# SyncE's loads in the order of their due times: a planner that lets transfers share one rate, on a four-phase transformer trunk

## The chip, the cores and the metric

The kernel runs on one core of a Trainium2 chip. The metric is the device time of one execution in microseconds (us). Before the change it is 1756.66 us, the median of three runs (1755.53 to 1757.88).

The core has five engines, which run side by side and wait for each other by semaphores: TensorE (PE in the profile; PEld is its loading of weights), VectorE (DVE), ScalarE (ACT), GpSimd (POOL) and SyncE (SP). Here SP computes nothing: it issues the loads of weights, one after the other. When a load has to wait for its buffer, every load behind it on SP waits too.

## The reference

The input x is 512 tokens of 1024 features. Two layers each apply an FFN at half weight, a mixer and another FFN at half weight; the mixer is gated linear attention (GLA) in layer 0 and stick-breaking attention (SB) in layer 1. At the end there is one more RMSNorm.

```python
def swiglu(h, w_gate, w_up, w_down):
    return (jax.nn.silu(h @ w_gate) * (h @ w_up)) @ w_down

for i in range(DEPTH):      # 2
    x = x + 0.5 * swiglu(rmsnorm(x, ffn1_norm[i]), ffn1_w_gate[i], ffn1_w_up[i], ffn1_w_down[i])
    h = rmsnorm(x, mix_norm[i])
    y = gla_mixer(h, ...) if i % 2 == 0 else sb_mixer(h, ...)
    x = x + y
    x = x + 0.5 * swiglu(rmsnorm(x, ffn2_norm[i]), ffn2_w_gate[i], ffn2_w_up[i], ffn2_w_down[i])
return rmsnorm(x, final_norm)
```

w_gate and w_up are 1024x2816, w_down is 2816x1024, all fp32. Four FFNs of 34.6 MB each, the mixers' weights and x make up the 175 MB that the kernel reads.

## The kernel before

**Data.** x stays in SBUF, transposed, as eight tiles x0 to x7 of 128 features x 512 tokens. Weights are loaded in fp32, most in chunks of 1 MB: `raw` (8x256 columns of 128 rows, or 4x512) for gate, up and the mixers, `rawd` (4x256 or 2x512, 512 KB) for the down projections. Each of these two names has two buffers: a load can go out once the tile two before it has been read for the last time.

**Products.** A product in fp32 precision is made of three faster ones. ACT casts a weight to its high part (`wh`, L527), DVE subtracts to get the low part (`wl`, L528), and TensorE adds up wh times the input's high part, wl times the high part and wh times the low part. Inputs are cut the same way (`nh`/`nl`, `hh`/`hl`, `xh`/`xl`, `th`/`tl`). Many products use a scheme of seven instead of eight block products (`seven`, L1069, for gate and up; `seven_down`, L736, for the down projection). It needs sums of weight blocks, made by DVE: `s12` and `s34` (L1079, L1080, L1085, L1086 from raw; L756, L757, L763, L764 from rawd). For the down projection DVE adds what TensorE has accumulated (`ps_w`, `ps_z`, `ps_q`) to x by L778; L727 does so for a plain down projection. TensorE can write on into a bank only after such a read. L950 makes the low part `sl` of the sum of squares of a norm, from which TensorE makes `ps_R` (L469).

**Program order and planned order.** The code emits instructions in an order of its own; a `Feed` walks through the products and calls `Chunk.load` (L486) for chunks ahead, by `nc.sync.dma_start` (L494). At the end a `Planner` (L49) sets a new order of each engine's instructions. `gather` (L81) collects instructions, what each depends on, and buffers; `price` (L171) gives each a duration (`cost`) and the time after which the engine can take the next (`step`). `due` (L271) works backwards from TensorE's instructions to a latest time (`late`) for every other instruction. `run` (L305) then plays the program forward: of all engines it takes the instruction that can start first and puts it at the end of that engine's list. For DVE and ACT the instruction is the one with the least `late` among those that can start by then; TensorE takes its program order, with a little skipping. SP and POOL keep the order of the program: `lists` holds it, and `choose` looks only at its head. `pin` (L55) keeps instructions of one engine in the order in which they are pinned. `begin`, at the start of the program, loads x and the first weights by SP (L2021, L2025, L2030).

The computed times only set orders. On the chip an instruction starts when its engine reaches it and its semaphores allow.

Of the kernel before, what the change touches and what calls it, by code (L numbers as in the profile page):

```python
# [48 lines left out]
class Planner:  # L49
# [5 lines left out]
    def pin(self, ins):  # L55
        e = str(ins.ins.engine)
        if e in self.pinned:
            self.behind_.append((self.pinned[e], ins.ins.name))
        self.pinned[e] = ins.ins.name
        return ins  # L60
# [110 lines left out]
    def price(self, i, kind, e, sizes, psum_in):  # L171
        n = max((s[1] for s in sizes), default=1)
        if e == "PE":
            types = [s[2] for s in sizes]
            if any("bfloat16" in t for t in types):
                return 270.0, max(64.0, 0.43 * n)
            if any("float32r" in t for t in types):
                return 165.0 + 0.42 * n, max(112.0, 0.422 * n)
            moving = sizes[0][1]
            full = sizes[1][1] == P and not kind.endswith("Transpose") and not getattr(i, "is_transpose", False)  # L180
            return 150.0 + 0.9 * n, max(58.0, 0.845 * moving) * (2 if full and moving in (1, P) else 1)
        if "DMA" in kind:
            total = max((s[1] * s[3] for s in sizes), default=1) * 4
            return 2000.0 + total / 400.0, 0.0
        scalars = sum(1 for s in sizes[:-1] if s[1] == 1 and n > 1)
        if e == "DVE":
            reads = [s for s in sizes[:-1] if s[1] > 1]
            if "Scan" in kind:
                n *= 2
            elif len(reads) == 1 and not psum_in and n > 256:  # L190
                n *= 0.5
            return 148.0 + 1.045 * n + 60.0 * scalars, 0.0
        if e == "Activation":
            if "Load" in kind:
                return 1290.0, 0.0
            return 190.0 + 0.835 * n + 95.0 * scalars - 30.0 * psum_in, 0.0
        return 200.0 + n, 0.0
# [107 lines left out]
    def run(self):  # L305
        self.gather()
        late = self.due()
        n = len(self.eng)
        left = [len(self.pred[k]) + self.held[k] for k in range(n)]
        ready, done = [0.0] * n, [None] * n  # L310
# [3 lines left out]
        got = set()  # L314
        clock = dict.fromkeys(ENGINES, 0.0)
        open_ = {e: set() for e in ENGINES}
        lists = {e: [k for k in range(n) if self.eng[k] == e] for e in ("SP", "Pool")}
        out = {e: [] for e in ENGINES}
        for k in range(n):
            if not left[k]:  # L320
                open_[self.eng[k]].add(k)
        shift = 0.0
        back = {"DVE": 80.0, "Activation": 100.0}

        def start(k):
# [13 lines left out]
        def choose(e):  # L339
            now = clock[e]  # L340
            if e in lists:
                if not lists[e] or left[lists[e][0]]:
                    return None
                s = start(lists[e][0])
                return None if s is None else (max(now, s), lists[e][0])
            if e == "PE":
                best = None
                for k in sorted(open_[e])[:60]:
                    s = start(k)
                    if s is not None:  # L350
                        if s <= now + 30.0:
                            return max(now, s), k
                        if best is None or s < best[0]:
                            best = (s, k)
                return best
            able = [(s, k) for k in open_[e] for s in (start(k),) if s is not None]
            if not able:
                return None
            t0 = max(now, min(able)[0])
            s, k = min((x for x in able if x[0] <= t0 + 1.0), key=lambda x: (late[x[1]], x[1]))  # L360
            d = self.cost[k] - back.get(e, 0.0)
            soon = [
                x for x in able
                if t0 + 1.0 < x[0] < t0 + 0.6 * d and late[x[1]] + shift < t0 + d and late[x[1]] < late[k]
            ]
            if soon:
                s, k = min(soon, key=lambda x: (late[x[1]], x[1]))
            return max(now, s), k

        for _ in range(n):  # L370
            best = None
            for e in ENGINES:
                c = choose(e)
                if c is not None and (best is None or c[0] < best[0]):
                    best = (*c, e)
            s, k, e = best
            out[e].append(k)
            open_[e].discard(k)
            if e in lists:
                lists[e].pop(0)  # L380
            end = done[k] = s + self.cost[k]
            if e == "PE":
                clock[e] = s + self.step[k] + (104.0 if s > clock[e] + 20.0 else 0.0)
                shift = s - late[k]
            elif "DMA" in type(self.ins[k]).__name__:
                clock[e] = s + (60.0 if e == "Activation" else 500.0)
            else:
                clock[e] = end - back.get(e, 0.0)
            for t in self.tiles[k]:
                c = self.tag[t]  # L390
                if t not in got:
                    got.add(t)
                    given[c] += 1
                    if used[c] < self.bufs[c]:
                        used[c] += 1
                    else:
                        heapq.heappop(freed[c])
                users[t] -= 1
                ends[t] = max(ends.get(t, 0.0), end)
                if not users[t]:  # L400
                    heapq.heappush(freed[c], ends[t])
            for b in self.succ[k]:
                if not e == self.eng[b] == "PE":
                    ready[b] = max(ready[b], end + self.lag(k, b))
            for b in self.succ[k] + self.after[k]:
                left[b] -= 1
                if not left[b]:
                    open_[self.eng[b]].add(b)
# [27 lines left out]
def decoder(ctx: ExitStack, tc: tile.TileContext, a: dict, out: bass.AP):  # L436
    nc = tc.nc
# [1556 lines left out]
    def begin(ip):  # L1994


        pin = plan.pin
# [14 lines left out]
        x0 = ip.tile([P, 4, NT, 256], F32, name="x0")  # L2012
        entries = {"g": feed.q[0], "u": feed.q[1], "q": feed.q[2]}
        raw = {}
# [3 lines left out]

        def load_x(qr):
            rows = a["x"][0].rearrange("(i p) d -> p i d", p=P)  # L2020
            nc.sync.dma_start(x0[:, qr], rows[:, :, qr * 256 : qr * 256 + 256])  # L2021

        def load_w(nm, hf):
            k = slice(hf * 4, hf * 4 + 4)
            nc.sync.dma_start(raw[nm][:, k], entries[nm].units[0][0].src[:, k])  # L2025

        load_x(0), load_w("g", 0), load_w("u", 0), load_x(1)
        load_x(2), load_w("g", 1), load_x(3), load_w("u", 1)
        for c in phases[0].lead[2:]:
            nc.sync.dma_start(c.t, c.src)  # L2030
        gains(1, ("mix_norm", "ffn2_norm", "gla_o_norm"))


# [141 lines left out]
        done = set()  # L2175
# [61 lines left out]
    with tc.tile_pool(name="ip", bufs=1) as ip:  # L2237
        begin(ip)
# [47 lines left out]
```

## Time and profile before

| | |
|---|---|
| median of three runs | 1756.66 us (1755.53 to 1757.88) |
| profiled execution, its own time | 1758.69 us |
| its span, first to last instruction | 1756.9 us |
| granted TensorE clock | 0.999 |
| PE busy | 1743.7 us, 99% |
| PEld busy | 1635.7 us, 93% |
| DVE busy | 1583.9 us, 90% |
| ACT busy | 1079.4 us, 61% |
| DMA queue of SP (q1) | 175.91 MB, 31.9% of 16 engines' time |

The profile is one execution with every instruction's start and end. A row such as `L528 DVE TENSOR_TENSOR wl<-raw,wh 128x1024 ... x241 | 255.4, 1062 | 50.1` gives line, engine, operation, tiles out and in (without their numbers), shape and count; then busy time in us, mean duration in ns, and the engine's idle time just before. In a timeline, the first two numbers are start and duration in us, and a bracket at the end gives idle time before the instruction and what ended it. A row of waits gives who waited for what: us in total, times, the longest one. For SP the time of an entry is the time of its issue alone, or, for several merged, from the first issue to the last. A row of DMA issues ends with the us from issue to landing. A row of windows gives a stretch, its length, each engine's busy time, the clock, the share of the DMA engines, and GB/s. The four FFNs take about 0 to 310, 520 to 850, 850 to 1170 and 1400 to 1750 us; GLA and SB lie between.

### The profile page before, as it was taken

To read this page: it belongs to the slowest core of one execution; us is meant where nothing else is said; L and a number is where in the kernel's file an instruction comes from. 1 tells how busy PE (TensorE), PEld (TensorE's weight loads), DVE (VectorE), ACT (ScalarE), POOL (GpSimd) and SP (SyncE) were. 2 spreads that over 40 slices of the span, in tenths; PEclk is the share of its full clock that TensorE was granted. 3 is DMA by queue.
4 is the path that set the end of the run, shared out by engine and by line. 5 is a ranking of instruction groups with operands and counts; after the bars stand their busy time and mean duration, and the time that the engine had idled before them with its cause. 6 is when DMAs were issued, how large, how long until landed. Compare 5 with 4: busy or idle time off the path is not lost.

```text
span 1756.9 us, 32000 instructions
## 1 busy us (share of the span) xinstructions
PE 1743.7 (99%) x13002; PEld 1635.7 (93%) x13002; DVE 1583.9 (90%) x2688; ACT 1079.4 (61%) x1906; POOL 9.9 (1%) x24
## 2 busy tenths in 40 slices
PE   9999999999999999999999999999999999999998
PEld 8999999899888899999989999999888888999997
DVE  8999999787888999999899999996898669899996
ACT  7556655545656566565656566566889755555655
POOL 0000000100000000000000000000000000000000
PEclk9999999999999999999999999999999999999999
DMA  6422423421233323333423324242222233233342
GB/s 192 132 85 73 150 85 116 142 73 51 72 96 96 120 71 122 116 101 121 140 75 98 126 92 132 85 132 73 61 73 74 71 96 120 83 111 118 100 132 73
DMA packets 178760, 179.30 MB, mean 102 GB/s; under 512 B 4082, under 2 KB 170276, under 8 KB 178612
## 3 DMA queue, kind: packets, MB, share of 16 engines
q1 hardware_dynamic: 177760, 175.91, 31.9%
q8 instruction: 102, 1.67, 0.4%
q0 software_dynamic: 608, 1.05, 0.3%
q14 instruction: 46, 0.38, 0.1%
q10 hardware_dynamic: 244, 0.29, 0.0%
HBM read 175.17 MB, written 2.10 MB: 101 GB/s over the span
## 4 chain that ended last, share of the span: by engine, by line
PE 78%; DVE 15%; DMA 2%; ACT 2%; issue 2%; DVEq 0%; ACTq 0%; SPq 0%
PE ps_w L1094 17%; PE ps_f L469 14%; PE ps_d L469 9%; PE ps_q L1094 9%; PE ps_w L772 5%; DVE wl L528 5%; PE ps_t L469 5%; PE ps_z L1094 4%; PE ps_b L469 4%; PE ps_q L772 3%; DVE x L778 2%; PE ps_z L1774 1%; PE ps_z L772 1%; DMA rawd<-in_ffn_w_down_dram 1%; PE ps_S L469 1%
## 5 line engine op out<-in xcount | busy, mean ns | idle before, releaser
L528 DVE TENSOR_TENSOR wl<-raw,wh 128x1024 fp32r<-128x1024 f32 x241 | 255.4, 1062 | 50.1 <-ACT wh L527 49.4
L527 ACT CAST wh<-s 128x1024 fp32r<-128x1024 f32 x192 | 201.6, 1051 | 141.2 <-DVE s L1080 38.3
L527 ACT CAST wh<-raw 128x1024 fp32r<-128x1024 f32 x241 | 221.7, 921 | 77.2 <-PE ps_f L469 26.7
L1094 PE MATMUL ps_w<-th,wh 128*128 128x256 f32 x864 | 238.3, 276 | 0.0
L528 DVE TENSOR_TENSOR wl<-s,wh 128x1024 fp32r<-128x1024 f32 x192 | 234.4, 1222 | 3.7 <-ACT wh L527 3.7
L1094 PE MATMUL ps_w<-th,wl 128*128 128x256 f32 x864 | 237.6, 275 | 0.0
L1094 PE MATMUL ps_w<-tl,wh 128*128 128x256 f32 x864 | 237.6, 275 | 0.0
L469 PE MATMUL ps_f<-xh,wh 128*128 128x512 f32 x432 | 166.4, 385 | 0.0
L1094 PEld LDWEIGHTS ps_w<-th,wh 128*128 128x128 f32 x864 | 165.8, 192 | 0.3
L1094 PEld LDWEIGHTS ps_w<-tl,wh 128*128 128x128 f32 x864 | 165.9, 192 | 0.0
L1094 PEld LDWEIGHTS ps_w<-th,wl 128*128 128x128 f32 x864 | 165.9, 192 | 0.0
L469 PE MATMUL ps_f<-xl,wh 128*128 128x512 f32 x432 | 163.7, 379 | 0.0
L469 PE MATMUL ps_f<-xh,wl 128*128 128x512 f32 x432 | 163.7, 379 | 0.0
L469 PE MATMUL ps_d<-hl,wh 128*128 128x512 f32 x288 | 109.4, 380 | 1.4 <-DVE hl L1192 1.4
L469 PE MATMUL ps_d<-hh,wh 128*128 128x512 f32 x288 | 109.8, 381 | 0.4 <-ACT hh L1191 0.2
L469 PE MATMUL ps_d<-hh,wl 128*128 128x512 f32 x288 | 109.2, 379 | 0.0
L527 ACT CAST wh<-rawd 128x512 fp32r<-128x512 f32 (+1 forms) x108 | 80.7, 766 | 20.9 <-PE ps_d L469 12.0
L528 DVE TENSOR_TENSOR wl<-rawd,wh 128x512 fp32r<-128x512 f32 (+1 forms) x108 | 92.9, 866 | 0.3 <-ACT wh L527 0.3
L469 PEld LDWEIGHTS ps_f<-xl,wh 128*128 128x128 f32 x432 | 81.6, 189 | 11.5
L469 PEld LDWEIGHTS ps_f<-xh,wh 128*128 128x128 f32 x432 | 81.7, 189 | 11.0
L469 PEld LDWEIGHTS ps_f<-xh,wl 128*128 128x128 f32 x432 | 81.7, 189 | 10.7
L1094 PE MATMUL ps_q<-th,wh 128*128 128x256 f32 x288 | 79.3, 275 | 0.0
(349 smaller groups left out, 5566.1 us busy)
## 6 DMA issues: line engine op xcount, KB each, us to landing
raw<-in_ffn_w_gate_dram SPq DMA_DIRECT2D x43, 1024.0 KB, 5.4
raw<-in_ffn_w_up_dram SPq DMA_DIRECT2D x43, 1024.0 KB, 5.6
rawd<-in_ffn_w_down_dram SPq DMA_DIRECT2D x84, 512.0 KB, 6.3
raw<-in_gla_w_in_dram SPq DMA_DIRECT2D x12, 1024.0 KB, 5.3
raw<-in_sb_w_in_dram SPq DMA_DIRECT2D x16, 512.0 KB, 3.9
raw<-in_gla_w_out_dram SPq DMA_DIRECT2D x4, 1024.0 KB, 5.1
raw<-in_sb_w_in_dram SPq DMA_DIRECT2D x4, 1024.0 KB, 5.1
raw<-in_sb_w_out_dram SPq DMA_DIRECT2D x4, 1024.0 KB, 5.9
```

The lines of the kernel that those rows point to most:

```text
L469: nc.tensor.matmul(ps, l, r, start=first, stop=last)
L527: nc.scalar.copy(h[:, k], part)
L528: nc.vector.tensor_tensor(out=l[:, k], in0=part, in1=h[:, k].bitcast(F32), op=ALU.subtract)
L772: st["pe"] = nc.tensor.matmul(ps, l_, r_, start=first and c + n == 0, stop=c == 1 and n == 2, skip_group_check=True).ins
L778: nc.vector.scalar_tensor_tensor(out=x, in0=ps, scalar=0.5, in1=x, op0=ALU.mult, op1=ALU.add)
L1094: st["pe"] = nc.tensor.matmul(o, l_, r_, start=first and j + n == 0, stop=j == 3 and n == 2, skip_group_check=True).ins
L1774: nc.tensor.matmul(o_, l_, r_, start=first, stop=last, skip_group_check=True)
```

## The change

Three things change in the planner, and the loads of `begin` are pinned.

- `price` gives a DMA of n bytes 2050 + n/318 ns instead of 2000 + n/400, and a step of n/318 ns instead of none. For 1 MB the cost goes from 4.6 us to 5.3 us.
- `run` lets SP's transfers share one rate: a load is done at the later of its own start plus cost and the end of the load before it plus its step (`bus`).
- `choose` takes for SP, as for DVE and ACT, the load with the least due time among those that can start. SP is no longer in `lists`; POOL is.
- The loads of x and of the first weights are pinned, so that their order stays.

```diff
         if "DMA" in kind:
             total = max((s[1] * s[3] for s in sizes), default=1) * 4
-            return 2000.0 + total / 400.0, 0.0
+            return 2050.0 + total / 318.0, total / 318.0
...
-        lists = {e: [k for k in range(n) if self.eng[k] == e] for e in ("SP", "Pool")}
+        lists = {"Pool": [k for k in range(n) if self.eng[k] == "Pool"]}
...
-        shift = 0.0
+        shift = bus = 0.0
...
             t0 = max(now, min(able)[0])
+            if e == "SP":
+                s, k = min((x for x in able if x[0] <= t0 + 1.0), key=lambda x: (late[x[1]], x[1]))
+                return max(now, s), k
...
             end = done[k] = s + self.cost[k]
+            if e == "SP":
+                end = done[k] = max(end, bus + self.step[k])
+                bus = end
...
-            nc.sync.dma_start(x0[:, qr], rows[:, :, qr * 256 : qr * 256 + 256])
+            pin(nc.sync.dma_start(x0[:, qr], rows[:, :, qr * 256 : qr * 256 + 256]))
...
-            nc.sync.dma_start(raw[nm][:, k], entries[nm].units[0][0].src[:, k])
+            pin(nc.sync.dma_start(raw[nm][:, k], entries[nm].units[0][0].src[:, k]))
...
-            nc.sync.dma_start(c.t, c.src)
+            pin(nc.sync.dma_start(c.t, c.src))
```

The program has the same instructions as before on every engine; their order differs. Of 232 entries on SP, 80 stand where they stood. Of DVE's 2685, 2183 do, of ACT's 1901, 1640, of TensorE's 12637, 12327. The order among the raw loads, and among the rawd loads, is kept; how the two are interleaved is new. In the changed file lines from 391 on stand six further down, so L494 becomes L500 and L778 becomes L784.

On SP in the first FFN, where four rawd loads in a row are followed by the raw loads of the next two chunks (numbers after the names tell tiles apart), before:

```order
L494 DMA raw_1083<-in_ffn1_w_gate_dram 128x8x256
L494 DMA rawd_1167<-in_ffn1_w_down_dram 128x4x256
L494 DMA rawd_1307<-in_ffn1_w_down_dram 128x4x256
L494 DMA rawd_1312<-in_ffn1_w_down_dram 128x4x256
L494 DMA rawd_1420<-in_ffn1_w_down_dram 128x4x256
L494 DMA raw_1425<-in_ffn1_w_up_dram 128x8x256
L494 DMA raw_1555<-in_ffn1_w_gate_dram 128x8x256
L494 DMA raw_1685<-in_ffn1_w_up_dram 128x8x256
```

and on SP at the same place after the change:

```order
L500 DMA raw_1083<-in_ffn1_w_gate_dram 128x8x256
L500 DMA rawd_1167<-in_ffn1_w_down_dram 128x4x256
L500 DMA raw_1425<-in_ffn1_w_up_dram 128x8x256
L500 DMA rawd_1307<-in_ffn1_w_down_dram 128x4x256
L500 DMA raw_1555<-in_ffn1_w_gate_dram 128x8x256
L500 DMA rawd_1312<-in_ffn1_w_down_dram 128x4x256
L500 DMA rawd_1420<-in_ffn1_w_down_dram 128x4x256
L500 DMA rawd_1954<-in_ffn1_w_down_dram 128x4x256
L500 DMA rawd_2075<-in_ffn1_w_down_dram 128x4x256
L500 DMA raw_1685<-in_ffn1_w_up_dram 128x8x256
```

raw_1425 and raw_1555 moved ahead of three and two rawd loads, and the next pair of rawd loads ahead of raw_1685. The other FFN stretches with seven-product down projections look alike.

On DVE in the last FFN, about 1534 to 1542 us of the profile, where the sums of a pair of rawd loads are followed by adds to x, before:

```order
L528 TENSOR_TENSOR wl_18102<-s34_18027,wh_18101 128x1024
L756 TENSOR_TENSOR s12_18107<-rawd_18105 128x512
L763 TENSOR_TENSOR s34_18155<-rawd_17997,rawd_18105 128x512
L757 TENSOR_TENSOR s12_18107<-s12_18107,rawd_17997 128x512
L528 TENSOR_TENSOR wl_18220<-rawd_17997,wh_18219 128x512
L778 SCALAR_TENSOR_TENSOR x4_85<-ps_q_18176,x4_85 128x256
L778 SCALAR_TENSOR_TENSOR x0_81<-ps_w_18158,x0_81 128x256
L778 SCALAR_TENSOR_TENSOR x5_86<-ps_q_18176,x5_86 128x256
L778 SCALAR_TENSOR_TENSOR x1_82<-ps_w_18165,x1_82 128x256
L528 TENSOR_TENSOR wl_18224<-s12_18107,wh_18223 128x1024
```

and on DVE at the same place after the change:

```order
L534 TENSOR_TENSOR wl_18102<-s34_18027,wh_18101 128x1024
L762 TENSOR_TENSOR s12_18107<-rawd_18105 128x512
L769 TENSOR_TENSOR s34_18155<-rawd_17997,rawd_18105 128x512
L763 TENSOR_TENSOR s12_18107<-s12_18107,rawd_17997 128x512
L784 SCALAR_TENSOR_TENSOR x0_81<-ps_w_18158,x0_81 128x256
L784 SCALAR_TENSOR_TENSOR x4_85<-ps_q_18176,x4_85 128x256
L784 SCALAR_TENSOR_TENSOR x1_82<-ps_w_18165,x1_82 128x256
L784 SCALAR_TENSOR_TENSOR x5_86<-ps_q_18176,x5_86 128x256
L534 TENSOR_TENSOR wl_18220<-rawd_17997,wh_18219 128x512
L534 TENSOR_TENSOR wl_18224<-s12_18107,wh_18223 128x1024
```

The four adds moved ahead of a wl, and the add from ps_w to their head. At other pairs the adds move further up, ahead of L763 and L757, which then stand behind them; a wl of the first rawd load moves ahead of L756.

On DVE at the head of the second FFN, about 550 to 555 us, where the norm's sum of squares is closed, before:

```order
L874 SCALAR_TENSOR_TENSOR ss_6270<-ss_6270,sq_6447 128x512
L885 SCALAR_TENSOR_TENSOR xl_6458<-x7_88,gT_78,xh_6457 128x512
L874 SCALAR_TENSOR_TENSOR ss_6270<-ss_6270,sq_6461 128x512
L528 TENSOR_TENSOR wl_6490<-raw_5983,wh_6489 128x1024
L950 TENSOR_TENSOR sl_6527<-ss_6270,sh_6525 128x512
```

and on DVE at the same place after the change:

```order
L880 SCALAR_TENSOR_TENSOR ss_6270<-ss_6270,sq_6447 128x512
L891 SCALAR_TENSOR_TENSOR xl_6444<-x6_87,gT_78,xh_6443 128x512
L880 SCALAR_TENSOR_TENSOR ss_6270<-ss_6270,sq_6461 128x512
L891 SCALAR_TENSOR_TENSOR xl_6458<-x7_88,gT_78,xh_6457 128x512
L956 TENSOR_TENSOR sl_6527<-ss_6270,sh_6525 128x512
L534 TENSOR_TENSOR wl_6490<-raw_5983,wh_6489 128x1024
```

sl and the last addition to ss moved up, past the wl of raw_5983. On TensorE, at the ends of the first three FFNs, one matmul of a plain down projection (ps_d<-hh,wh) moved 73 matmuls further back. On ACT, early in the second FFN, the cast wh<-raw that follows wh<-s moved ahead of a cast hh<-t.

## The prediction

> **What bounds the kernel now.** I began with the busy times of the page, then took the idle time of TensorE, then looked for what ends it.
>
> ```profile
> PE 1743.7 (99%) x13002; PEld 1635.7 (93%) x13002; DVE 1583.9 (90%) x2688; ACT 1079.4 (61%) x1906; POOL 9.9 (1%) x24
> ```
>
> TensorE is busy for 1743.7 of 1756.9 us. The change neither adds nor removes an instruction, so the only thing that it can give back is TensorE's waiting: 13.2 us of idle time in all, of which the first matmul's wait and the tail after the last matmul (outputs) are not touched by any load. What the profile blames on data in between is little:
>
> ```profile
> PE ps_w L772 <- DVE x L778: 1.8, 2, 1.5
> PE ps_d L469 <- DVE hl L1192: 1.4, 2, 1.0
> ...
> PE ps_R L469 <- DVE sl L950: 0.4, 1, 0.4
> ...
> PE ps_q L772 <- DVE x L778: 0.2, 1, 0.2
> ```
>
> (Columns: total us, times, longest.) No row says that TensorE waits for a DMA. Loads reach it through ACT and DVE, which split each fp32 weight tile into a high and a low part. In an FFN, DVE has almost no room:
>
> ```profile
> 21.00:310.00 289.00, 288.95 (x2306) 280.38 (x2306) 281.20 (x481) 172.46 (x307) 1.04 (x1) 1.00 0.34 106
> ```
>
> In 289 us DVE is busy 281.2, so a DVE wait of one or two us is not made up before TensorE needs the result. The waits of DVE and ACT for loads in the body of the program are these, but for a few us:
>
> ```profile
> DVE s L756 <- DMA rawd<-in_ffn_w_down_dram: 8.8, 8, 2.7
> ...
> ACT wh L527 <- DMA raw<-in_ffn_w_up_dram: 9.1, 4, 3.3
> ```
>
> ACT, busy for 61%, waits for raw loads at the start and at the heads of FFNs, where a load goes out as soon as its buffer is free. DVE has eight waits, one at each pair of down-projection loads that feed L756. The longest, 2.7 us, is followed by the longest wait of TensorE:
>
> ```profile
> 1534.12 1.23 DVE L528 TENSOR_TENSOR wl<-s,wh 128x1024 fp32r<-128x1024 f32 x1 [0.66 <-ACT wh L527]
> 1538.05 0.69 DVE L756 TENSOR_TENSOR s<-rawd 128x512 f32<-128x512 f32 x1 [2.70 <-DMA rawd<-in_ffn_w_down_dram]
> 1538.66 0.69 DVE L763 TENSOR_TENSOR s<-rawd 128x512 f32<-128x512 f32 x1
> 1539.26 0.69 DVE L757 TENSOR_TENSOR s<-s,rawd 128x512 f32<-128x512 f32 x1
> 1539.86 0.68 DVE L528 TENSOR_TENSOR wl<-rawd,wh 128x512 fp32r<-128x512 f32 x1
> 1540.46 0.42 DVE L778 SCALAR_TENSOR_TENSOR x<-ps_q,x 128x256 f32<-128x256 f32 x1
> 1540.80 0.41 DVE L778 SCALAR_TENSOR_TENSOR x<-ps_w,x 128x256 f32<-128x256 f32 x1
> ```
>
> TensorE needs the second of these L778 adds (it reads ps_w, into which the next product goes), and goes on at 1541.27, just after it ends at 1541.21.
>
> **The loads.** SP's queue in program order holds a blockade:
>
> ```profile
> 84.87 33.04 SPq L494 DMA_DIRECT2D rawd<-in_ffn_w_down_dram  x4
> 117.97 0.50 SPq L494 DMA_DIRECT2D raw<-in_ffn_w_up_dram  x1
> 118.52 0.82 SPq L494 DMA_DIRECT2D raw<-in_ffn_w_gate_dram  x1
> ```
>
> Four rawd loads wait one after the other for their two buffers, from 84.87 to 117.9, and two raw loads stand behind them. In the new queue raw_1425 and raw_1555 stand between the rawd loads, so each goes out when its own buffer is free. That is far earlier, but nobody waited for these two: no row of DVE's waits names a raw load of the FFN body, and ACT's four are elsewhere. The rawd pair itself (rawd_1312, rawd_1420) goes out when it did, because its buffers, not the queue, hold it. What it loses is company:
>
> ```profile
> raw<-in_ffn_w_gate_dram SPq DMA_DIRECT2D x1, 1024.0 KB, 10.9
> rawd<-in_ffn_w_down_dram SPq DMA_DIRECT2D x1, 512.0 KB, 4.5
> ...
> rawd<-in_ffn_w_down_dram SPq DMA_DIRECT2D x1, 512.0 KB, 6.8
> ...
> rawd<-in_ffn_w_down_dram SPq DMA_DIRECT2D x1, 512.0 KB, 3.7
> ```
>
> (Issue to landing: the first two were issued from 117.5 to 118.9, the third at 1531.27, the last alone at 303.81.) The later raw loads pay most for the sharing; the rawd load takes 4.5 at the usual place, 6.8 at the bad one, 3.7 alone. So I give the shorter landing by itself between 0 and 3.1 us (6.8 to 3.7) at the bad place, and nothing at the other seven, where the adds of L778 were in time but for one.
>
> **The gain comes from DVE's order.** The plan now believes that a pair of rawd loads lands later than it used to think, and so it puts L778 adds ahead of work that can wait. At 1540 the add of ps_w moves from behind wl and the add of ps_q to the front of the group: 0.60 (start to start, 1539.86 to 1540.46) and 0.34 (1540.46 to 1540.80), together 0.94 us earlier, even if the load is as late as here. What one such wait costs is read from the starts of matmuls:
>
> ```profile
> 1539.47 0.28 PE L772 MATMUL ps_z<-hl,wh 128*128 128x256 f32 x1
> 1541.27 0.38 PE L772 MATMUL ps_w<-nh,wh 128*128 128x256 f32 x1 [1.52 <-DVE x L778]
> 1541.48 0.28 PE L772 MATMUL ps_w<-nh,wl 128*128 128x256 f32 x1
> ...
> 1551.35 0.28 PE L772 MATMUL ps_w<-t,wh 128*128 128x256 f32 x1
> 1551.93 0.38 PE L772 MATMUL ps_w<-nh,wh 128*128 128x256 f32 x1 [0.31 <-DVE x L778]
> 1552.15 0.28 PE L772 MATMUL ps_w<-nh,wl 128*128 128x256 f32 x1
> ```
>
> Undisturbed, 256-column matmuls start 0.11 us apart. Here 1.80 and 0.21 stand in place of 0.11 twice: 1.79 us lost, 0.27 more than the 1.52 shown. At 1551.93 it is 0.58 and 0.22, so 0.58 lost; there the add of ps_w that is waited for also moves ahead, past a 1.2 us wl. The ps_q wait of 0.24 costs 0.24 and the same 0.27: 0.51. **Term 1: 1.79 + 0.58 + 0.51 = 2.9 us**, with 0.6 of it left (1.52 less 0.94) if the load is late again.
>
> Term 2 is the norm at the head of the second FFN, where sl moves ahead of a 1.2 us wl split of raw_5983:
>
> ```profile
> 554.01 0.38 PE L469 MATMUL ps_f<-xh,wh 128*128 128x512 f32 x1
> 554.78 0.48 PE L469 MATMUL ps_R<-sl,one_r 128*128 128x512 f32 x1 [0.39 <-DVE sl L950]
> 555.10 0.38 PE L469 MATMUL ps_f<-xh,wl 128*128 128x512 f32 x1
> ```
>
> 512-column matmuls start 0.22 apart (0.11 for half the columns, doubled); 0.77 and 0.32 stand here, so **0.65 us**, all gained if sl is 0.4 earlier, and it moves by up to 1.2.
>
> Term 3: at three places (about 302, 839 and 1160) a matmul ps_d<-hh,wh is moved 73 matmuls later, some 8 us, past the point at which its freshly split weight made it late:
>
> ```profile
> 301.64 0.28 PE L1094 MATMUL ps_w<-nl,wh 128*128 128x256 f32 x1
> 301.96 0.48 PE L469 MATMUL ps_d<-hh,wh 128*128 128x512 f32 x1
> 302.28 0.27 PE L1094 MATMUL ps_q<-th,wh 128*128 128x256 f32 x1
> ```
>
> 0.32 for 0.11, and 0.32 for 0.22: 0.31 each, **0.9 us** for three, if the next matmul in line is ready; nothing if it is not. I take it whole.
>
> Against these stands one cast that I find moved the wrong way:
>
> ```profile
> 592.42 0.61 ACT L1191 CAST hh<-t 128x512 fp32r<-128x512 f32 x1
> 592.95 1.04 ACT L527 CAST wh<-raw 128x1024 fp32r<-128x1024 f32 x1
> ```
>
> The wh cast now comes first, so hh ends some 0.94 us later (1.04 less the overlap of 0.1 by which ACT's instructions run into each other). TensorE waits soon after for the hl made from it anyway, so I book 0.25, a restart; the bounds are 0 and 0.94. Elsewhere the DVE and ACT lists change by local swaps of under 2 us, and I book them at nothing.
>
> Sum: 2.9 + 0.65 + 0.9 - 0.25 = 4.2 us of the profiled execution, 1758.69 to 1754.5. That execution lies 2.03 above the median of 1756.66. If the 6.8 us landing was its bad luck, terms of 1.79 + 0.58 are absent from the median run, and it gains only 1.8, to 1754.8. If the 2.03 is the price of profiling, the median gains 4.2, to 1752.5. One landing of 6.8 where 4.5 is usual speaks for luck; I go nearer to that end: **1754.0 us**.
>
> **A rule weighed.** The row of 10.9 us above is a load issued behind three others, twice the page's median of 5.4 for its kind. The Trainium skill, in DMA: Bandwidth & Descriptors (Queues, rings and completion order), says that each DMA engine takes the descriptors of a ring in their order, so whatever stands ahead on SP's queue is paid by what follows; the trace agrees. By that rule a raw load put ahead of an urgent rawd load is a danger, and this is the second rival.
>
> **The rivals.** *Hidden anyway:* the raw loads were never waited for, DVE is as full as before (281 of 289 us), and each wait removed comes back at another place, or was luck. For it: DVE's busy work is the same to the instruction. Against it: the adds that TensorE waited for move ahead. Time: 1756.66 less at most 1, 1755.5 to 1757.4. Chance 0.24.
>
> *Slower by a load put ahead.* At the end of three FFNs the two first loads of the mixer now stand ahead of the last two rawd loads:
>
> ```profile
> 303.81 4.64 SPq L494 DMA_DIRECT2D rawd<-in_ffn_w_down_dram  x2
> 308.50 1.20 SPq L494 DMA_DIRECT2D raw<-in_gla_w_in_dram  x2
> ...
> 298.75 1.23 DVE L528 TENSOR_TENSOR wl<-raw,wh 128x1024 fp32r<-128x1024 f32 x1
> ...
> 309.23 1.05 ACT L527 CAST wh<-rawd 128x1024 fp32r<-128x1024 f32 x1 [1.01 <-PE ps_q L1094]
> ```
>
> The second of them gets its buffer from the DVE row that ends at 299.98, the rawd load could go at 303.81: 3.8 us of margin. If DVE slips by more than that, the rawd load goes out behind a fresh 1 MB. Half a MB costs 5.4 less 3.7, 1.7, so 1 MB costs 3.4; the load landed at 307.5 and was first read at 309.23, 1.7 of slack; 1.7 late, and 0.27 for the restart, at three places: 5.9 us, 1762.6, or 1759.9 if the gains on the median of about 2.7 stay: 1761. At the heads of three FFNs two rawd loads stand ahead of a raw load in the same way; there the raw load waits for its own buffer for most of the time that they take. Against it: DVE waits 2.7 us at most for a load in this profile, less than 3.8. Chance 0.06.
>
> *More than this:* the two hl waits (1.4 us and two restarts, 1.9) go as well. DVE's list is all but unchanged ahead of the longer of them, so this needs luck: 1750.5 to 1752.5. Chance 0.10.
>
> **How the numbers follow.** My forecast, 1752.5 to 1755.5, has 0.60. A run of this kernel is told from no change at about 0.2%, 3.5 us: below 1753.15 is faster, above 1760.2 slower. Of the forecast 0.25 lies below 1753.15, and all of the third rival: faster 0.35. Slower 0.06. The rest, 0.59, is within the bound. The range runs from 1751.6 (inside the third rival) to 1757.4 (the whole of the first).
>
> **What would show it.** Right: no L772 row among TensorE's waits, or under 0.6 us in all; ps_R gone from them; the blockade of 33 us gone from SP's queue, and the raw loads near 5.4 us to landing; L756 still waiting for its loads, for the buffers are the same. The sum fails at term 1 if waits on L778 come back at other pairs, at term 3 if TensorE shows 0.3 us steps at about 302, 839 and 1160 still. All of it is wrong if ACT or DVE waits for a rawd load near 309, 847 or 1167, or if TensorE waits for over 6 us in all.

## The result, and the profile after

| | before | after |
|---|---|---|
| median of the runs | 1756.84 us (8 runs, 1755.53 to 1758.52) | 1751.37 us (8 runs, 1751.02 to 1752.67) |
| ratio, 95% interval | | 0.9969 [0.9959, 0.9979] |
| profiled execution | 1758.69 us, span 1756.9 | 1751.15 us, span 1749.2 |
| granted TensorE clock | 0.999 | 0.999 |

The changed kernel is 5.5 us faster, 0.31%. The forecast was 1754.0 and its range began at 1751.6: the sign is right, but the gain is twice the forecast's 2.7, and the time fell just below the range.

Busy times and the chain that ended last, on the page of the changed kernel. (All lines from L390 on are six higher than before.)

```profile
PE 1738.9 (99%) x13002; PEld 1634.5 (93%) x13002; DVE 1585.5 (91%) x2688; ACT 1079.5 (62%) x1906; POOL 9.9 (1%) x24
...
PE 91%; DVE 6%; ACT 1%; issue 1%; DMA 1%; DVEq 0%; SPq 0%; ACTq 0%
```

DVE's and ACT's work is what it was; the chain now runs 91% over TensorE and 6% over DVE (78% and 15% before). TensorE's waits (total us, times, longest):

```profile
PE ps_f L2066 <- DVE gT L467: 0.9, 1, 0.9
PE ps_oT L1865 <- ACT wt L998: 0.7, 1, 0.7
PE ps_q L778 <- DVE x L784: 0.4, 1, 0.4
PE ps_x L2073 <- DMA x<-in_x_dram: 0.4, 1, 0.4
PE ps_f L2082 <- ACT xh L2118: 0.4, 1, 0.4
PE ps_b L475 <- DVE r L1836: 0.3, 1, 0.3
PE ps_f L2082 <- DVE wl L2139: 0.2, 1, 0.2
PE ps_w L778 <- ACT ps_z L796: 0.2, 1, 0.2
```

The waits for x into ps_w (1.8), for sl (0.4) and, against the forecast, for hl (1.4) are all gone from this list. What is new is small: 0.4 for x into ps_q, at 187.53, 0.2 for ACT, and 1.0 in the first 20 us, for x, xh and wl. Then three views of the loads: the waits of ACT and DVE for them, SP's queue in the stretch of the old blockade (start, duration), and the issues of rawd (count, KB, median us to landing):

```profile
ACT wh L533 <- DMA raw<-in_ffn_w_up_dram: 4.9, 2, 3.3
DVE s L762 <- DMA rawd<-in_ffn_w_down_dram: 3.1, 6, 1.2
```
```profile
84.42 0.37 SPq L500 DMA_DIRECT2D rawd<-in_ffn_w_down_dram  x1
92.00 0.37 SPq L500 DMA_DIRECT2D raw<-in_ffn_w_up_dram  x1
98.54 0.37 SPq L500 DMA_DIRECT2D rawd<-in_ffn_w_down_dram  x1
106.85 0.37 SPq L500 DMA_DIRECT2D raw<-in_ffn_w_gate_dram  x1
116.47 0.97 SPq L500 DMA_DIRECT2D rawd<-in_ffn_w_down_dram  x2
```
```profile
rawd<-in_ffn_w_down_dram SPq DMA_DIRECT2D x84, 512.0 KB, 3.5
```

The blockade of 33 us in SP's queue is gone: raw loads go out between the rawd loads. The median rawd load lands after 3.5 us instead of 6.3, and DVE waits 3.1 us for them instead of 8.8. All this is as the forecast said it would show, L756 (now L762) still waiting included. One thing that it had named as a sign against its first term is there too: the wait for an add of x at 187.53, at a pair that had none before.

**Where the time went.** For each matmul that has one and the same name in both programs I took its start before minus its start after, the *lead*. It ends at 7.7 us (the profiled executions differ by 7.5) and rises in steps. Those of over 0.5 us:

| time before, us | step, us | what TensorE waited for | forecast |
|---|---|---|---|
| 302, 840, 1160 | +0.57, +0.55, +0.56 (each followed by up to -0.22) | wh, freshly cast | 0.31 each |
| 556 | +0.86 | sl | 0.65 |
| 596 | +0.71 | hl | -0.25 |
| 1132 | +0.51 | x (ps_q) | 0.51 |
| 1468 | +1.41 | hl | 0 |
| 1540, 1552 | +1.79, +0.58 | x (ps_w) | 1.79, 0.58 |
| 188 | -0.65 | x (ps_q), new | 0 |

The places that the forecast named are there with about its sizes. Two that it did not give, 596 and 1468, are the heads of the second and the fourth FFN, and hold 2.1 us. But a step in a pair of single executions may be chance. The experiments have to say which of these steps every execution has, and what makes them.

### The profile page after: what moved, and what is told of

Same layout as the page of the kernel before. It is cut to its first block, busy times and chain, and to the rows that moved or that the text cites. A ratio compares the mean times of both kernels' runs of the same rounds, so it can differ in the third digit from the quotient of the medians.

```text
span 1749.2 us, 32041 instructions
## 1 busy us (share of the span) xinstructions
PE 1738.9 (99%) x13002; PEld 1634.5 (93%) x13002; DVE 1585.5 (91%) x2688; ACT 1079.5 (62%) x1906; POOL 9.9 (1%) x24
## 4 chain that ended last, share of the span: by engine, by line
PE 91%; DVE 6%; ACT 1%; issue 1%; DMA 1%; DVEq 0%; SPq 0%; ACTq 0%
PE ps_w L1100 21%; PE ps_f L475 15%; PE ps_d L475 11%; PE ps_q L1100 10%; PE ps_w L778 7%; PE ps_z L1100 5%; PE ps_t L475 5%; PE ps_b L475 5%; PE ps_q L778 3%; DVE wl L534 2%; PE ps_z L778 2%; PE ps_z L1780 1%; PE ps_S L475 1%; PE ps_bt L475 1%; PE ps_oT L1865 1%; PE ps_T L1850 1%
```

## The experiments

**Lists** is the theory that the gain sits in the new orders of TensorE, VectorE and ScalarE, **landings** that it sits in loads that land sooner, because SP's queue is in another order. Behind these stands the finer question which lists. The planner can be run with any of its three new rules left out, and each engine's order taken from either run:

```diff
-    def run(self):
+    def plan(self, rate, share, due_order):   # new price, one shared rate, SP by due time
...
+    def run(self):
+        new = self.plan(True, True, True)[0]
+        old = self.plan(False, False, False)[0]
```

Planned this way, the price and the shared rate without the due times give exactly the changed kernel's lists on the three engines, and the due times without them give exactly the lists of before. (This is read from the orders that the planner makes; neither setting was run by itself.) So the change falls into two halves that do not touch each other. (In the experiments all lines are a few higher again, by the lines that were added. Pairs of numbers in their diffs are first and last position in an engine's list.)

### The two halves

```diff
+        out = {**old, "SP": new["SP"]}      # loads alone
+        out = {**new, "SP": old["SP"]}      # lists alone
```

> SyncE's queue in the new order, the lists of TensorE, VectorE and ScalarE as before. Theory 'lists' (that of the prediction): the gain sits in VectorE's and TensorE's lists, and shorter landings help at most at the one bad load near 1540. Then 1755.0 to 1757.0 us, with TensorE still waiting for hl (1.4 us in 2 waits), for sl (0.4) and showing the 0.3 us steps at 302, 839 and 1160. Theory 'landings': loads that land sooner leave VectorE without the idle times of 1.79 us near 1435 and 0.67 us near 560 and with 1.2 instead of 2.7 us near 1540, and TensorE's waits for hl and for x fall away behind them: 1.41 + 0.71 + 1.79 + 0.58 = 4.5 us, so about 1752.4 us. Under 'landings' the wait for sl (0.65 lost) and the three steps stay.

> The new lists of TensorE, VectorE and ScalarE, SyncE's queue in program order as before. Theory 'lists': 1751.4 to 1752.5 us, all or nearly all of the gain of 5.5. Theory 'landings': only what a list can give with loads as late as before: the wait for sl (0.65), the three steps (0.9), the swap of the adds near 1540 (1.2 of 1.79, and 0.58), 3.3 us, so about 1753.5 us or, where the lists now count on loads that come later than they think, more.

Loads alone: 1756.25 us in 11 runs against 1757.43, ratio 0.9993 [0.9984, 1.0001]. Lists alone: 1752.43 in 6 runs, ratio 0.9971 [0.9959, 0.9982]. Nearly all of the gain is in the lists. The new queue of loads, and with it the due times, has no gain of its own that can be told from noise. With loads alone the waits for hl stay, as the lists theory said, and the way in which they stay refutes the landings theory at its main place. First the kernel before, at the head of the fourth FFN, in the timelines of SP, ACT, DVE and TensorE:

```profile
1429.15 0.37 SPq L494 DMA_DIRECT2D raw<-in_ffn_w_up_dram  x1
1429.57 1.12 SPq L494 DMA_DIRECT2D rawd<-in_ffn_w_down_dram  x2
...
1435.76 1.05 ACT L527 CAST wh<-raw 128x1024 fp32r<-128x1024 f32 x1 [2.76 <-DMA raw<-in_ffn_w_up_dram]
...
1436.83 1.23 DVE L528 TENSOR_TENSOR wl<-raw,wh 128x1024 fp32r<-128x1024 f32 x1 [1.79 <-ACT wh L527]
1437.97 0.68 DVE L1231 TENSOR_TENSOR t<-ps_f,R 128x512 f32<-128x512 f32 x1
...
1470.77 0.48 PE L469 MATMUL ps_d<-hl,wh 128*128 128x512 f32 x1 [0.97 <-DVE hl L1192]
```

The up load takes 6.6 us from issue to first use. ACT waits for it, DVE's wl waits for ACT, and the norm's t, which needs no load, stands behind wl. DVE loses 1.79 us, is full for the next 33 us, and TensorE meets the loss at 1470.77. I had blamed the two rawd loads right behind the up load. With loads alone they go out ahead of it, and have landed (at 1427.4) when it starts:

```profile
1419.55 1.12 SPq L508 DMA_DIRECT2D rawd<-in_ffn_w_down_dram  x2
1428.13 0.37 SPq L508 DMA_DIRECT2D raw<-in_ffn_w_up_dram  x1
...
1434.78 1.05 ACT L541 CAST wh<-raw 128x1024 fp32r<-128x1024 f32 x1 [2.81 <-DMA raw<-in_ffn_w_up_dram]
...
1435.86 1.23 DVE L542 TENSOR_TENSOR wl<-raw,wh 128x1024 fp32r<-128x1024 f32 x1 [1.84 <-ACT wh L541]
...
1469.80 0.48 PE L483 MATMUL ps_d<-hl,wh 128*128 128x512 f32 x1 [0.98 <-DVE hl L1206]
```

Alone on the queue, it takes 6.6 us all the same, and the wait is unchanged. Its late landing has another cause (last section).

### The heads of the FFNs

```diff
+        # the up load behind the two rawd loads, at three heads
+        for e, a, b in (("SP", 71, 73), ("SP", 115, 117), ("SP", 183, 185)):
+        # VectorE: wl behind norm operations, at two heads
+        for e, a, b in (("DVE", 864, 871), ("DVE", 2160, 2163)):
+            out[e][a : b + 1] = new[e][a : b + 1]     # the rest of out is old
```

> The kernel before, with one change: at the heads of three FFNs the two down-projection loads go ahead of the up-projection load that stood in front of them. Theory 'landings': that up-projection load then lands 5.4 us after its issue near 1429 instead of 6.6, VectorE idles 0.6 instead of 1.79 us there, and TensorE's wait for hl near 1470.8 (1.0 us, with its restart 1.4) is gone, as is that near 596 (0.7): about 1754.7 us. Theory 'lists': the waits for hl stay as they are, 1756.8 us.

> The kernel before, with one change on VectorE alone: at the heads of two FFNs (near 560 and 1436) the split wl of the late up-projection weights stands behind three or four norm operations that are ready, instead of ahead of them. Theory 'backlog' (a VectorE idle time is carried to TensorE by a full list, whatever causes it): the three operations of 0.6 us fill the 1.79 us of idle time although the load lands as late as before, and TensorE's waits for hl near 596 and 1470.8 fall away: 1.4 + 0.7 us, about 1754.7 us. If only the landing counts: idle time moves behind the three operations, the waits for hl stay, 1756.8 us.

Loads moved: 1756.24 us, ratio 0.9996 [0.9987, 1.0005]. Order moved: 1756.31, ratio 0.9993 [0.9984, 1.0002]. Neither time can be told from no change, so the traces decide. Loads moved: the up load lands after 5.3 us, DVE idles 0.57 instead of 1.79, the lead rises by 1.16 at 1468 and by nothing at 596. That looks like the expected gain, but loads alone had the same queue there and a late load: it was a draw. Order moved, in the timelines of SP, ACT and DVE:

```profile
1428.58 0.37 SPq L513 DMA_DIRECT2D raw<-in_ffn_w_up_dram  x1
1429.00 1.12 SPq L513 DMA_DIRECT2D rawd<-in_ffn_w_down_dram  x2
...
1434.04 1.05 ACT L546 CAST wh<-raw 128x1024 fp32r<-128x1024 f32 x1 [1.62 <-DMA raw<-in_ffn_w_up_dram]
...
1435.79 0.74 DVE L1204 SCALAR_TENSOR_TENSOR xn<-x,gT,R 128x512 f32<-128x512 f32 x1
1436.45 1.22 DVE L547 TENSOR_TENSOR wl<-raw,wh 128x1024 fp32r<-128x1024 f32 x1
```

Here the up load landed on time with the two rawd loads right behind it, the mirror image of loads alone. DVE does not idle, and TensorE's wait for hl near 1470 is gone, +1.63. What the order is worth against a late load shows in a second profile of the changed kernel, which met one:

> The changed kernel itself once more, to stand beside the two runs sent with it. 1751.0 to 1752.0 us, 5.5 below the kernel before. If the gain were luck of a few executions, it would come out nearer to 1754.

```profile
1432.05 1.05 ACT L533 CAST wh<-raw 128x1024 fp32r<-128x1024 f32 x1 [2.92 <-DMA raw<-in_ffn_w_up_dram]
...
1431.29 0.69 DVE L1237 TENSOR_TENSOR t<-ps_f,R 128x512 f32<-128x512 f32 x1
1431.90 0.68 DVE L1244 TENSOR_TENSOR t<-ps_f,R 128x512 f32<-128x512 f32 x1
1432.50 0.74 DVE L1191 SCALAR_TENSOR_TENSOR xn<-x,gT,R 128x512 f32<-128x512 f32 x1
1433.16 1.22 DVE L534 TENSOR_TENSOR wl<-raw,wh 128x1024 fp32r<-128x1024 f32 x1
...
1465.72 0.48 PE L475 MATMUL ps_d<-hl,wh 128*128 128x512 f32 x1 [0.28 <-DVE hl L1198]
```

(Timelines of ACT, DVE and TensorE.) ACT waits 2.92 us, as long as before (2.76), and DVE not at all: three norm operations of 0.6 us have filled the time. The kernel came to 1751.63 us in 5 runs, ratio 0.9968 [0.9955, 0.9980], so the gain repeats. Thirteen traces, sorted by list and by the load's time from issue to first use, with the time lost at the matmuls that wait near 1468 (start to start over the usual, restart of 0.1 left out):

| | load late (6.5 to 6.8 us) | load on time (5.3 to 5.6 us) |
|---|---|---|
| old list on VectorE | 1.53, 1.59, 1.54, 1.44 | 0.51, 0.64, 0.60, 0.61 |
| new list on VectorE | 0.63, 0 (no sharing), 0.44 | 0.27, 0 |

(The fourteenth, the last try below, has a list of its own; its load took 6.5 us, and it lost nothing here.)

At the second head, by contrast, order moved on VectorE alone gave only +0.15 at 596. Two more runs asked why:

```diff
+        # VectorE and ScalarE at the second head
+        for e, a, b in (("DVE", 849, 888), ("Activation", 547, 580)):
+        # VectorE alone at the second head
+        for e, a, b in (("DVE", 849, 888),):
```

> The kernel before, with the lists of VectorE and ScalarE as in the changed kernel at one place alone, the head of the second FFN (about 545 to 582), and without the swap of the casts hh and wh near 592. Theory 'heads': the wait for sl at 554.8 (0.65 lost) and that for hl at 594.8 (0.6 to 0.7 lost) both go, 1.3 us: about 1756.0 us. VectorE alone did not do it (0.15 at 594.8), so the order on ScalarE would be what was missing: v ahead of the cast wh. Rival: the swap of the casts near 592 takes the wait for hl away, and here it stays.

> The second head (545 to 582) with VectorE's new list alone, ScalarE's as before. Theory 'both engines': ScalarE still makes the cast wh ahead of v, so VectorE's v waits 3.3 us there (1.5 with both lists, 2.8 + 0.7 at two places before); sl ahead of wl takes TensorE's wait near 554.8 away (0.65 to 0.85), the wait for hl near 594.8 stays at 0.3 to 0.6: about 1756.0 us. Rival: VectorE's list is enough, both waits go, 1.3 to 1.5 us: about 1755.4 us.

Both engines: 1754.79 us, ratio 0.9990 [0.9981, 0.9999]; steps of +0.83 at 556 and +0.71 at 596, the very steps of the change. VectorE alone: 1755.29, ratio 0.9990 [0.9980, 1.0000]; +0.88 and only +0.15. DVE's idle times at that head, from its timelines before, with VectorE alone, and with both:

```profile
557.52 1.23 DVE L528 TENSOR_TENSOR wl<-raw,wh 128x1024 fp32r<-128x1024 f32 x1 [2.80 <-ACT wh L527]
560.75 1.23 DVE L528 TENSOR_TENSOR wl<-raw,wh 128x1024 fp32r<-128x1024 f32 x1 [0.67 <-ACT wh L527]
```
```profile
557.37 0.69 DVE L981 SCALAR_TENSOR_TENSOR v<-ps_R,v 128x512 f32<-128x512 f32 x1 [2.35 <-ACT v L980]
```
```profile
558.13 0.69 DVE L982 SCALAR_TENSOR_TENSOR v<-ps_R,v 128x512 f32<-128x512 f32 x1 [1.52 <-ACT v L981]
```

VectorE's new list asks for v first, and ScalarE's old list makes a cast of 1.03 us before v, as the timeline of ScalarE with VectorE's list alone shows:

```profile
555.78 1.03 ACT L545 CAST wh<-raw 128x1024 fp32r<-128x1024 f32 x1
556.71 0.62 ACT L980 ACTIVATE v<-R 128x512 f32<-128x512 f32 x1
```

So ScalarE's swap is part of the gain: one engine's list alone moves the idle time to the next instruction. The step at 596 is 0.71 in all six traces with both lists there, and 0.15 in the two with VectorE's alone. (I had expected 3.3 us there; 2.35 is what came, since with sl moved ahead a wl of 1.22 us runs within that time.)

> The changed kernel with the lists of VectorE (and ScalarE at the second FFN) as before at the heads of two FFNs, 545 to 582 and 1430 to 1437. Theory 'heads': the waits for sl near 551 (0.8) and for hl near 591 (0.7) come back, and that for hl near 1466 (0.3 to 1.4, with the landing of the load before it); 1.8 to 2.9 us slower than the change: 1753.2 to 1754.3 us. Rival: with the loads in order of due time the lists at the heads do not matter any more, within 0.5 us of the change.

```diff
+        # the change, with the old lists at two heads
+        for e, a, b in (("DVE", 849, 888), ("Activation", 547, 580), ("DVE", 2160, 2163)):
+            out[e][a : b + 1] = old[e][a : b + 1]     # the rest of out is new
```

1754.57 us in 11 runs, beside 1751.63 for the change on the same chip; ratio to before 0.9986 [0.9977, 0.9995]. The lead falls by 0.93, 0.53 and 0.28 between 552 and 724 and by 2.06 between 1456 and 1464. With the load late, the wait for hl is there as before (0.97 at 1469.13). Undoing the heads costs 2.9 us by the medians, of a gain of 5.0 on this chip. In the trace, though, 0.76 of the 2.06 goes at four matmuls from a wait for nh on:

```profile
1457.04 0.48 PE L489 MATMUL ps_f<-nh,wh 128*128 128x512 f32 x1 [0.19 <-ACT nh L1211]
```

A gate load took 6.2 us there, and ScalarE's nh stood behind its cast. Neither the kernel before nor the change loses time at this place, so it may be a draw of this one execution. All traces together give the heads less, 2.1 us (in the section on why the prediction was right, and where it was wrong).

### The terms of the forecast

> The change without the shared rate: loads have the new, higher price and go out by due time, but each is believed to move at its own rate. VectorE's and ScalarE's lists then have the changes at the heads of the FFNs (norm operations ahead of wl, sl ahead of wl), but not the adds of x ahead of wl near 1540, and TensorE's list is that of before. Theory 'heads' (most of the gain comes from the heads of the FFNs): 0.65 + 0.7 + 1.0 to 1.6 us there and about 1 from the loads, so 1753.5 to 1754.5 us; the 0.3 us steps at 302, 839 and 1160 and the wait for x near 1550 stay. Theory 'adds and steps' (the terms of the prediction): what is left out carries the gain, 1756.0 to 1757.0 us.

```diff
+        out = self.plan(True, False, True)[0]     # new price and due times, no shared rate
```

1753.24 us in 11 runs, ratio 0.9979 [0.9970, 0.9988]. Its lists have the changes at the heads, but neither the moved matmuls nor the adds near 1540. Steps: +0.83 at 556, +0.71 at 596, +1.74 at 1468 (with a load that lands late, 6.5 us); none at 302, 840, 1160 and 1552. So the price, without the shared rate, sets the heads right. The shared rate adds the rest, 1.6 to 1.9 us by medians that were not measured side by side.

> The kernel before, with the one matmul moved 73 places later at each of three places (302, 839, 1160) and nothing else. The prediction gave 0.31 us for each, 0.9 in all: about 1756.4 us, with the lead rising by 0.3 at each place. Rival: the next matmul in line is not ready either, or the moved one waits at its new place: no step.

```diff
+        for e, a, b in (("PE", 2325, 2397), ("PE", 6107, 6179), ("PE", 8557, 8629)):
+            out[e][a : b + 1] = new[e][a : b + 1]     # the rest of out is old
```

1755.32 us, ratio 0.9993 [0.9984, 1.0002]. Steps at the three places: +0.58 then -0.21; +0.55 then -0.73, where a new wait of 0.35 for ACT's o appears at 842.3; +0.56 then -0.22. Net 0.37, -0.18 and 0.34. The size of one is right, the middle one is given back.

> The kernel before, with VectorE's list as in the changed kernel at one place alone, from 1538 to 1552, where adds of x move ahead of wl splits. The prediction gave this place 1.79 + 0.58 us, and 1.2 of the 1.79 for the adds even if the load is late. If the late load near 1531 was chance (5.2 us from issue to landing in three other runs, 6.8 in the profile of before), the wait near 1540 is 0.1 to 0.6 us in most runs, and the gain is 0.6 to 1.1: about 1756.4 us; TensorE's wait for x near 1550 is gone in either case.

```diff
+        for e, a, b in (("DVE", 2316, 2320), ("DVE", 2327, 2338)):
+            out[e][a : b + 1] = new[e][a : b + 1]     # the rest of out is old
```

1757.27 us, ratio 1.0002 [0.9993, 1.0011]: no gain to be seen in the time, though the interval would still hold one of 1.2 us. Three kernels with the old queue here, near 1540, in the timelines of DVE and TensorE: the one with three moved matmuls (old adds), this one (new adds), and the one with loads moved at the heads (old adds):

```profile
1534.63 0.69 DVE L776 TENSOR_TENSOR s<-rawd 128x512 f32<-128x512 f32 x1 [2.77 <-DMA rawd<-in_ffn_w_down_dram]
...
1537.86 0.38 PE L792 MATMUL ps_w<-nh,wh 128*128 128x256 f32 x1 [1.59 <-DVE x L798]
```
```profile
1538.66 0.69 DVE L775 TENSOR_TENSOR s<-rawd 128x512 f32<-128x512 f32 x1 [2.74 <-DMA rawd<-in_ffn_w_down_dram]
...
1540.94 0.38 PE L791 MATMUL ps_w<-nh,wh 128*128 128x256 f32 x1 [0.63 <-DVE x L797]
```
```profile
1535.06 0.69 DVE L776 TENSOR_TENSOR s<-rawd 128x512 f32<-128x512 f32 x1 [1.11 <-DMA rawd<-in_ffn_w_down_dram]
...
1538.28 0.38 PE L792 MATMUL ps_w<-nh,wh 128*128 128x256 f32 x1
```

A late load costs TensorE 1.59 us with the old adds and 0.63 with the new, which is the 0.6 of the forecast. With the load on time there is no wait to remove. And what this kernel gains here (+0.90, and +0.58 at 1552), it gives back by 1620 (-0.24, -0.52, -0.46, -0.13, -0.20), in part to a wait for ACT's o at 1560.5 of 0.25. The whole change loses 0.4 there. What else in its lists saves the difference was not tried.

How often is this load late? With the old queue at this place, issue to landing took 6.8, 5.2, 5.6, 5.7, 6.8, 6.8, 4.7 and 5.2 us in eight kernels. With the new queue, which has no raw load 0.4 to 1.2 us behind it, it took 4.8 to 5.3 in six. This is what the order of loads does by itself: six traces with old adds and old queue lose 1.69, 0.09, 0.56, 0.66, 1.75 and 0.13 us near 1540 (0.8 on average), and loads alone loses 0.15. That agrees with the 1.2 us of its medians, whose interval reaches to zero.

### A try to go on

> The changed kernel with one number of the price of a load raised, 2650 in place of 2050 ns, so that the lists count on landings that come 0.6 us later, half of the 1.2 us by which some loads land late. If the lists still suffer from late landings, 0.3 to 0.8 us faster than the change: about 1751.0 us. If TensorE's remaining waits (3.5 us, of which only 0.3 near 1465 hangs on a load's landing in the body) have other causes, within 0.5 us of the change; and if splits are now put off too far, new waits for wh or wl and 1752 to 1753 us.

```diff
-            return 2050.0 + total / 318.0, total / 318.0
+            return 2650.0 + total / 318.0, total / 318.0
```

1752.43 us in 8 runs, beside 1751.63: not faster. The waits that were left in the FFNs, at 187, 1118 and 1465, are gone from its trace. But that execution lost 1.7 us in its first 9 us against the change's; its full clock began at 10.2 us, and that of the change's at 3.8 (last section). Whether a price in between is worth a few tenths stays open.

## Why the prediction was right, and where it was wrong

**Right: what bounds the kernel and what carries the gain.** TensorE's few waits, not the loads themselves. The lists alone give 5.1 of the 5.5 us.

**What each place is worth on average.** For this I took the time between the same two matmuls, as the mean of the traces that have the old lists there (5 to 8) less the mean of the three with all the new lists (the change twice, lists alone). The heads give 2.1 us (0.7 at 556, 0.7 at 596, 0.6 at 1468), the places at 1541 and 1552 1.4, and the three moved matmuls 1.0. Another 1.3 us lies between 120 and 295, 605 and 830, and 865 and 1110: no term named it, and no run took it apart. Some 0.6 is lost, most of it near 188. The sum is 5.3 without the first 15 us, beside the 5.0 to 5.5 of the medians.

**Term 1 (2.9 us): right place, mixed in kind.** The wait at 1552 is steady: eight traces with old adds show it at 0.47 or 0.48 before the restart, and those with new adds show 0 to 0.14. The wait at 1541 is a lottery of 0.1 to 1.75 us, 1.7 in the profile of before. I called both bad luck and so absent from the median run. The 0.58 is always there, and the lottery costs 0.8 on average, which the new queue and the new adds end. The 0.51 at 1132 was chance: kernels with the old lists there show the same step. And 0.65 us of the term (0.4 on average) is lost again at 188, where an add of x now comes late: the same wait of 0.4 stands in the second profile of the change, in lists alone and with the heads undone, so it belongs to the new lists.

**Term 2 (0.65): right,** 0.83 to 0.88 by the lead, 0.7 on average.

**Term 3 (0.9): right in size for two of three.** Alone, the middle one gives its gain back to a wait for ACT at 842; in the whole change it does not.

**The steps that failed** are the last ones of the sum: the swap at 592 was booked at minus 0.25, and all other local swaps of DVE and ACT at nothing. The runs showed +0.7 at 596 and +0.6 on average at 1468 (1.41 in the profiled pair) in their place.

**Minus 0.25 at 592: the first of them.** I priced one swap of casts by its direct neighbour. DVE's hl there waits behind a full list, not for that cast. With both engines' lists at the head the wait at 596 goes (+0.71) without that swap, and the change, which has it, gains the same +0.71. It costs nothing.

**"DVE's list is all but unchanged ahead of the longer of them, so this needs luck": the second.** The two hl waits were read from where they end. The list is all but unchanged in the 33 us ahead of 1470, and the loss was made before that, at 1435, where one wl stood ahead of three norm operations. "Elsewhere the DVE and ACT lists change by local swaps of under 2 us, and I book them at nothing" is this error in general form. A swap of 1.2 us beside an idle time of DVE is worth the idle time, as long as DVE stays full up to TensorE's next need. And ACT's waits for raw loads at the heads, which I dismissed as waits of an engine that is busy for 61%, are where the idle time came from. The third rival named the right waits, with a chance of 0.10 and a time of 1750.5 to 1752.5 that holds the result.

**Luck or price of profiling.** Luck is the better reading: the profile of before holds both late loads. And no price of profiling shows: in the thirteen other runs the profiled execution lies between 1.4 us below the run's median and 2.9 above it, and the three that lie furthest above are those whose full clock began after 10 us. But from luck I concluded that the median gains only 1.8. All runs of before scatter from 1754.5 to 1761.3 us, and those of the change from 1751.0 to 1752.7. A kernel whose waits are drawn by lot loses their mean, and a list that takes a late load calmly gains it.

**The rivals.** Nothing was slower by a raw load put ahead: neither ACT nor DVE waits for a rawd load at the three FFN ends. "Hidden anyway" holds for the loads and not for the lists.

## What to carry to other kernels

Where one full engine feeds the bound one, follow a wait back along the full engine's list to its last idle time, however far back, and ask what ready work stands behind the instruction that idles there. A planner's durations matter most through that: a load believed 0.7 us too early puts its consumer ahead of work that is ready. Lists on several engines belong together: undo or try them together, or the idle time only moves by one instruction. And take several traces before calling a wait of one execution a term or an accident; some are drawn anew each time, and then their mean is what a change can win.

## What the runs showed of the hardware

**Late loads go with instruction fetches.** The page of before lists, among the DMA queues:

```profile
q8 instruction: 102, 1.67, 0.4%
```

These are fetches of 16 KB each, and q14 has more of 8 KB. In the fourteen traces I took all gate and up loads of 1 MB that had SP's queue to themselves. Of 436 with no fetch under way between 1.2 and 4.5 us after their issue, two took over 5.8 us (median 5.3). Of 78 with one, 35 did, at 5.9 to 6.7. The up load at the head of the fourth FFN was late in all five traces where the fetch began 3.7 to 4.25 us after its issue, on time in all five where it began after 4.5, and late in three of four in between. So an instruction fetch that falls into a load can go with 0.6 to 1.4 us more, and a few tenths in the phase of the two decide it. No run moved a fetch on purpose, so that it is the cause is inferred. The late rawd load near 1531 is another case, and its cause stays open: in all eight traces with the old queue a fetch began 0.2 to 0.9 us before that load, whether it was late or not.

**The price of a load.** Alone on the queue, 1 MB takes 5.3 us here and 512 KB 3.4 (rawd) to 3.8 (raw), by the medians. The Trainium skill, in DMA: Bandwidth & Descriptors (Anatomy of one DMA), fits 2.0 us plus bytes over 436 GB/s for loads issued by another engine, which would be an estimate of 4.4 us for 1 MB; the traces say 5.3 for these.

**The clock at the start is drawn by lot.** TensorE's first 512-column matmuls, before, and with both engines' lists at the second head:

```profile
7.83 0.38 PE L2076 MATMUL ps_f<-xh,wl 128*128 128x512 f32 x1
8.05 0.38 PE L2076 MATMUL ps_f<-xl,wh 128*128 128x512 f32 x1
```
```profile
8.18 0.63 PE L2095 MATMUL ps_f<-xh,wl 128*128 128x512 f32 x1
8.61 0.63 PE L2095 MATMUL ps_f<-xl,wh 128*128 128x512 f32 x1
```

They start 0.22 us apart in one execution and 0.43 in the other, with the same list there, and the second loses 1.4 us by 10 us. The Trainium skill, in TensorE: Matmul & The Clock Gate (Part 1, the HAM clock gate), says that the array starts at half clock until a free-running window of 3.4 us has been busy, so that the point varies from run to run; these rows agree. So do the traces' own records of the clock: the full clock begins 3.8 to 6.7 us after the start in eleven executions and 10.2 to 10.5 us after it in three, the second one above among them. With one execution of each kernel, such a step must not be read as a gain or a loss.
